# Weights stored block by block in order of use, and a fifth row of the memory output projection opened in the second score buffer

## The chip, the cores and the metric

The kernel runs on one core of one Trainium2 chip. The metric is the device time of one execution in microseconds (us), lower is better. A core has TensorE (PE, matrix products; PEld is its loading of the stationary operand), VectorE (DVE), ScalarE (ACT), GpSimd (POOL) and SyncE (SP), which here only issues transfers (DMAs) from the chip's memory (DRAM) to on-chip memory and back. Matrix products go into eight PSUM buffers of 128 x 512 float32.

## What is computed

Two layers of an encoder over 512 tokens of width 1024, with 256 memory tokens beside them. Each layer adds three things to x, and a last RMS norm follows:

```python
x = x + hybrid_mixer(rms_norm(x, norm_mix[l]), w_in[l], na_rpb[l],
                     gqa_q_norm[l], gqa_k_norm[l], w_out[l], rows, cos, sin)
x = x + memory_cross_attention(rms_norm(x, norm_mem_q[l]), rms_norm(mem, norm_mem_kv[l]),
                               w_mem_q[l], w_mem_kv[l], w_mem_o[l])
x = x + conv_ffn(rms_norm(x, norm_ffn[l]), w_up[l], conv_w[l], conv_b[l], w_down[l])
```

The mixer projects with w_in (1024 x 2304), runs eight heads of neighbourhood attention on an 8 x 64 grid and eight query heads of grouped attention over all tokens, and projects with w_out. The memory part is

```python
q = (h @ w_q).reshape(b, s, MEM_HEADS, MEM_HEAD_DIM)
sc = jnp.einsum('bqhd,bmhd->bhqm', q, k, preferred_element_type=jnp.float32) * (MEM_HEAD_DIM ** -0.5)
p = jax.nn.softmax(sc, axis=-1)
o = jnp.einsum('bhqm,bmhd->bqhd', p.astype(v.dtype), v).reshape(b, s, MEM_WIDTH)
return o @ w_o
```

with four heads of width 128, so the output projection sums over four k-steps of 128, one for each head. The feed-forward part projects to 2 x 2816 columns (w_up), convolves over three positions, gates, and projects back (w_down). Everything is float32.

## The kernel before

x is kept transposed, as eight tiles of 128 features x 512 tokens ("xT"). Each float32 factor is split into a high part and a low part in a reduced format (float32r), and a product is made of three: high x high, high x low, low x high (`mm3`, `gemm_T`). A 128 x 128 x 512 product is therefore three PE instructions of 512 columns.

**Weights.** `plan` lists all weight blocks in the order of their use, each with its DRAM source, its number of k-steps and of columns. A block is 512 KB (448 KB for blocks of w_down of seven k-steps). `emit_raw` loads it into one of two "raw" buffers (N_RAW) on SP's queue; `emit_split` makes the parts: ACT copies the high one ("hi<-raw"), POOL or DVE subtracts for the low one ("lo<-raw,hi"). Four pairs of hi and lo stand at a time (N_W). A raw buffer is free for the next load when its low part is made, so the load of a block goes out behind the split of the block two ahead of it. In DRAM the weights lie as the reference has them (w_in with reordered columns), and a block is cut out of a matrix: `cols` takes rows k0*128 on and columns c0 on, so one k-step of one partition is a piece of 512 B (128 columns), 1 KB (256) or 2 KB (512), and pieces follow each other at the pitch of the matrix: 9216 B for w_in, 22528 B for w_up, 4096 B for w_down and w_mem_kv. The four "outg" blocks of w_out are loaded in two halves of 64 partitions.

**The opening.** The first three weight blocks and x are loaded in slices (`FIRST`, `first_loads`): k-step 0 and 1 alone, then two k-steps at a time, with x's chunks between them, so that PE can start on the first slices. The two first slices of weights are issued by ACT, all else by SP.

**The memory part.** `mem_rows` makes the output projection: eight rows (128 output features x 512 tokens), each the sum of four k-steps, one for each head's output mo[0] to mo[3]. PSUM has four buffers named "mm", two named "sc" (scores) and two named "tr". While the heads are still worked on, rows 0 to 2 (N_ROWS = 3) are opened in "mm" buffers and get k-steps 0 to 2 as the heads become ready; row 3 is opened in an "sc" buffer. Then `mem_rows` waits for mo[3] (ACT copies its high part out of PSUM, DVE makes the low part). After that it walks over the rows: an opened row gets its last k-step, the others are opened in a free "mm" buffer and get all four. `Norm.close` then adds the row to xT, and makes the operands of the feed-forward part ("xg") and their squares, on DVE, ACT and POOL. Two rows share one block of w_mem_o.

**The order of the work.** The program is not issued as written. All calls go onto a tape (`Tape`, `Step`); a planner (`Tape.plan`, `run`, `due`) simulates it with a duration for each step, chooses an order for each engine among the steps that can start, and takes the best of nine such orders under small random delays. PE's order may differ from the tape by up to 300 of its own steps. `play` then issues the chosen order, and each engine executes its own list in that order. For a DMA the planner assumes 450 ns of issue, 1800 ns to land, and a transfer rate in `Step.__init__`: 205 GB/s for fewer than 128 partitions or within SBUF, 285 where a piece (the last dimension) is under 1 KB, 340 otherwise. Since all calls are issued from `play`, every instruction has the line of `take` or `play` in the profile (L376), and groups are told apart by their tiles.

Of the kernel before, what the change touches and what calls it, by code (L numbers as in the profile page):

```python
# [19 lines left out]
P = 128  # L20
# [48 lines left out]
    return n  # L69


def tag_of(tensor):
    return re.sub(r"(_\d+)+$", "", tensor.name)


class Step:
# [394 lines left out]
def encoder_kernel(ctx: ExitStack, tc: tile.TileContext, t: dict, out: list):  # L471
# [51 lines left out]


    def raw_tile():
        key, loads, nk, ncol, eng = plan[len(raws)]
# [5 lines left out]
        return raw, loads  # L532

    def emit_raw():
        raw, loads = raw_tile()
        for dst, src in loads:
            SP.dma_start(dst(raw), src)

    def emit_split(act=ACT, cuts=2):
        n = len(ready)  # L540
        key, loads, nk, ncol, eng = plan[n]
        raw = raws[n]
        raws[n] = None
        if key[0] in ("up", "down", "memq", "memo"):
            cuts = 1
        if eng[1:] == "r":
            hi, lo = rtile((nk, ncol)), rtile((nk, ncol))
        else:
            hi = wpool.tile([P, nk, ncol], F32R, tag="hi", name=nm("hi"))
            lo = wpool.tile([P, nk, ncol], F32R, tag="lo", name=nm("lo"))  # L550
        for i in range(cuts):
            k = slice(nk * i // cuts, nk * (i + 1) // cuts)
            act.copy(hi[:, k], raw[:, k])
            (POOL if eng[0] == "P" else DVE).tensor_sub(lo[:, k], raw[:, k], f(hi)[:, k])
        ready.append((hi, lo))
# [22 lines left out]
    def plan_up(l, j):  # L578
        cols(("up", j, 0), t["w_up"][l], 0, KC, P * j, P)
        cols(("up", j, 1), t["w_up"][l], 0, KC, D_FF + P * j, P)  # L580

    def plan_down(l, g):
        j0, nj = GROUPS[g]
        if l + 1 < DEPTH or g + 1 < len(GROUPS):
            for m in range(KC):
                cols(("down", g, m), t["w_down"][l], j0, nj, P * m, P)
            return
        for n, (k0, c0) in enumerate(((0, 0), (2, 0), (4, 0), (6, None), (0, 512), (2, 512), (4, 512))):
            eng = "P" if n < 2 else "Pr"
            if c0 is None:  # L590
                cols(("down", g, n), t["w_down"][l], j0 + k0, 1, 0, D, eng)
            else:
                cols(("down", g, n), t["w_down"][l], j0 + k0, 2, c0, 512, eng)

    def plan_wide(name, w, c0, eng="PPPP"):
        for kq in range(4):
            cols((name, kq), w, 2 * kq, 2, c0, 512, eng[kq])

    def plan_layer(l):
        w_in, w_out = t["w_in"][l], t["w_out"][l]  # L600
        for n, p in NA_ORDER:
            if n == "v":
                plan_wide("v", w_in, 1024, "DPDP")
            else:
                eng = {("q", 0): "Dx", ("k", 0): "Dx", ("q", 1): "Dx"}.get((n, p), "P") if l == 0 else "P"
                cols((n, p), w_in, 0, KC, (0 if n == "q" else 512) + P * p, P, eng)
        for kh in range(2):
            cols(("gkv", kh), w_in, 4 * kh, 4, 2048, 256)
        plan_wide("gq", w_in, 1536)
        for mp in range(4):  # L610
            cols(("outn", mp), w_out, 0, 4, 256 * mp, 256, "P")
        for m in range(4):
            cols(("memk", m), t["w_mem_kv"][l], 0, KC, P * m, P)
        plan_wide("memv", t["w_mem_kv"][l], 512)
        for mp in range(4):
            c = slice(256 * mp, 256 * mp + 256)
            plan.append((("outg", 0, mp), [
                (lambda r: r[0:64], w_out[512:768, c].rearrange("(k p) c -> p k c", p=64)),
                (lambda r: r[64:128], w_out[768:1024, c].rearrange("(k p) c -> p k c", p=64)),
            ], 4, 256, "P"))  # L620
        for h in range(4):
            cols(("memq", h), t["w_mem_q"][l], 0, KC, P * h, P)
        for mp in range(4):
            cols(("memo", 0, mp), t["w_mem_o"][l], 0, 4, 256 * mp, 256)
        for g, (j0, nj) in enumerate(GROUPS):
            for j in range(j0 + (g > 0), j0 + nj):
                plan_up(l, j)
            if g + 1 < len(GROUPS):
                plan_up(l, j0 + nj)
            plan_down(l, g)  # L630

    for l in range(DEPTH):
        plan_layer(l)

    def get_wide(name):
        return [get_w((name, kq), min(AHEAD, 3 - kq)) for kq in range(4)]
# [27 lines left out]
    for n in FIRST:  # L664
        if isinstance(n, slice):
            to = slice(n.start, n.stop + (n.stop == S))
            SP.dma_start(xg0[0][:, to], t["xT"][0:P, to])
        elif isinstance(n, int):
            SP.dma_start(xg0[n], t["xT"][n * P : (n + 1) * P, :])
        else:  # L670
            u, k0, nk = n
            if u == len(first_loads):
                first_loads.append(raw_tile())
            raw, loads = first_loads[u]
            (ACT if u < 2 and k0 == 0 else SP).dma_start(raw[:, k0 : k0 + nk], loads[0][1][:, k0 : k0 + nk])
# [172 lines left out]
    def mem_stat():  # L848

        acc = None  # L850
        for i in range(KC // 2):
            sq = tmp((2, MEMN))
            SP.dma_start(sq, t["memT"][i * 256 : (i + 1) * 256, :].rearrange("(k p) n -> p k n", p=P))
# [46 lines left out]
    for l in range(DEPTH):  # L900
# [560 lines left out]
        def mem_rows():  # L1461
# [231 lines left out]
    return np.ascontiguousarray(tab.astype(np.float32))  # L1693


def _in_order():

    order = _head_order()
# [58 lines left out]
```

## Time and profile before

| | |
|---|---|
| median of 3 runs | 1324.64 us (1323.74 to 1324.8) |
| profiled execution | 1324.17 us, of which the span is 1322.3 us |
| read from DRAM, written | 126.18 MB, 2.10 MB |
| packets of the hardware queue q1 | 197,808 with 135.84 MB |
| instructions | 17,751, of which 6,373 PE products |

Durations and times in the prediction come from the one profiled execution, and its times count from the span's start. In a row of a timeline the columns are start, duration, engine, operation, tiles written and read, shapes and count, and in brackets the idle time of the engine ahead of it with what ended it. "x3" means that three such instructions in a row are shown as one. A PE product's duration is from its start until its result has passed the array, so several overlap; the distance from one start to the next is what PE needs for each. In rows of waits the numbers are total us, times, and the longest.

### The profile page before, as it was taken

How to read it: one execution, taken by the hardware profiler on the slowest of the kernel's cores; microseconds unless marked ns; L12 is line 12 of the kernel's file. 1: busy time of each engine (PE TensorE's matmuls, PEld its weight loads, DVE VectorE, ACT ScalarE, POOL GpSimd, SP SyncE). 2: the span in 40 equal slices, each digit the busy share in tenths (PEclk: the TensorE clock that was granted, in tenths of full speed). 3: DMA queues.
4: the chain of work that ended last, by engine and by line, in shares of the span. 5: the costliest groups of instructions: out<-in, count | busy, mean ns of one | idle time of the engine just before them, and what ended most of it. 6: DMA issues, size and time to landing. Idle time of an engine off the chain costs nothing.

```text
span 1322.3 us, 17751 instructions
## 1 busy us (share of the span) xinstructions
PE 1313.2 (99%) x6373; PEld 1105.8 (84%) x6373; DVE 936.4 (71%) x1657; ACT 675.2 (51%) x1229; POOL 691.9 (52%) x481
## 2 busy tenths in 40 slices
PE   9999999999999999999999999999999999999998
PEld 7898888888888888888888988888888888888897
DVE  7679896776994488178445898866779835862875
ACT  6777786555442244144447867855644423432441
POOL 3565866726544444444636657775455444444451
PEclk9999999999999999999999999999999999999999
DMA  8661313322333333342355522233133333323331
GB/s 248 192 184 49 112 58 87 96 62 82 112 96 96 96 96 91 103 123 81 89 168 168 144 64 80 71 89 96 49 112 104 99 100 96 92 84 111 96 112 64
DMA packets 198327, 137.29 MB, mean 104 GB/s; under 512 B 5216, under 2 KB 185056, under 8 KB 198240
## 3 DMA queue, kind: packets, MB, share of 16 engines
q1 hardware_dynamic: 197808, 135.84, 35.1%
q8 instruction: 51, 0.84, 0.3%
q10 hardware_dynamic: 432, 0.33, 0.1%
q14 instruction: 36, 0.29, 0.1%
HBM read 126.18 MB, written 2.10 MB: 97 GB/s over the span
## 4 chain that ended last, share of the span: by engine, by line
PE 97%; ACT 1%; DVE 1%; POOL 0%; DMA 0%; issue 0%; SPq 0%; DVEq 0%; POOLq 0%; ACTq 0%
PE mm L376 86%; PE sc L376 6%; PE tr L376 4%; POOL lo L376 0%; DMA xT<-in_xT 0%; ACT hi L376 0%; ACT xg L376 0%; ACT t L376 0%; DVE r L376 0%; ACT r L376 0%; SPq L376 0%; DVE xg L376 0%; DVE t L376 0%; POOL t L376 0%; DVE s L376 0%
## 5 line engine op out<-in xcount | busy, mean ns | idle before, releaser
L376 POOL TENSOR_TENSOR lo<-raw,hi 128x1024 fp32r<-128x1024 f32 (+2 forms) x268 | 512.3, 1922 | 481.6 <-ACT hi L376 450.7
L376 PE MATMUL mm<-xg,hi 128*128 128x512 f32 (+1 forms) x1730 | 535.6, 390 | 0.8 <-ACT hi L376 0.8
L376 ACT CAST hi<-raw 128x512 fp32r<-128x512 f32 (+2 forms) x276 | 226.2, 839 | 354.7 <-PE mm L376 329.1
L376 PEld LDWEIGHTS mm<-xg,hi 128*128 128x128 f32 x1730 | 322.5, 188 | 65.9 <-ACT hi L376 1.0
L376 PE MATMUL mm<-xg,lo 128*128 128x512 f32 (+1 forms) x865 | 336.7, 389 | 0.0
L376 PE MATMUL mm<-r,hi 128*128 128x512 f32 (+1 forms) x1056 | 333.0, 390 | 0.4 <-ACT r L376 0.4
L376 DVE SCALAR_TENSOR_TENSOR t<-t,par,t 128x504 f32<-128x504 f32 (+1 forms) x352 | 281.3, 837 | 38.5 <-ACT t L376 36.5
L376 PEld LDWEIGHTS mm<-r,hi 128*128 128x128 f32 x1056 | 197.2, 188 | 40.3 <-ACT r L376 1.3
L376 PE MATMUL mm<-r,lo 128*128 128x512 f32 (+2 forms) x560 | 210.8, 376 | 0.0
L376 PEld LDWEIGHTS mm<-xg,lo 128*128 128x128 f32 x865 | 162.4, 188 | 33.7
L376 PEld LDWEIGHTS mm<-r,lo 128*128 128x128 f32 x560 | 105.2, 188 | 19.5
L376 DVE TENSOR_TENSOR xT<-xT,mm 128x512 f32<-128x512 f32 (+1 forms) x56 | 37.1, 667 | 111.8 <-PE mm L376 111.5
L376 PE MATMUL mm<-hi,xg 128*128 128x512 f32 (+1 forms) x384 | 107.7, 357 | 0.0
L376 POOL TENSOR_SCALAR t<-t,s 128x512 f32<-128x512 f32 (+1 forms) x112 | 66.7, 610 | 59.0 <-DVE s L376 52.5
L376 DVE TENSOR_TENSOR t<-mm,rep 128x512 f32<-128x512 f32 x88 | 60.1, 687 | 35.4 <-PE mm L376 35.2
L376 PE MATMUL sc<-r,r 128*128 128x256 f32 (+1 forms) x382 | 83.7, 336 | 0.0
L376 ACT ACTIVATE t<-sc,s,s 128x512 f32<-128x512 f32 (+1 forms) x96 | 67.9, 711 | 26.4 <-DVE s L376 25.0
L376 ACT ACTIVATE t<-t,par 128x512 f32<-128x512 f32 x88 | 70.8, 810 | 15.8 <-DVE t L376 15.8
L376 PEld LDWEIGHTS mm<-hi,xg 128*128 128x128 f32 x384 | 68.5, 189 | 9.4
L376 PE MATMUL tr<-ident,t 128*128 128x128 f32 x488 | 70.8, 272 | 0.3 <-POOL lo L376 0.3
L376 PEld LDWEIGHTS tr<-ident,t 128*128 128x128 f32 x488 | 59.3, 140 | 11.8 <-issue 0.8
L376 PE MATMUL mm<-lo,xg 128*128 128x512 f32 (+1 forms) x192 | 68.0, 356 | 0.0
(125 smaller groups left out, 1510.3 us busy)
## 6 DMA issues: line engine op xcount, KB each, us to landing
raw<-in_w_up SPq DMA_DIRECT2D x88, 512.0 KB, 3.9
raw<-in_w_in SPq DMA_DIRECT2D x33, 512.0 KB, 4.3
raw<-in_w_down SPq DMA_DIRECT2D x23, 512.0 KB, 4.0
raw<-in_w_down SPq DMA_DIRECT2D x24, 448.0 KB, 3.7
raw<-in_w_mem_kv SPq DMA_DIRECT2D x16, 512.0 KB, 4.0
r<-r SPq DMA_DIRECT2D x30, 256.0 KB, 3.5
r<-in_bias SPq DMA_DIRECT2D x16, 384.0 KB, 5.7
raw<-in_w_out SPq DMA_DIRECT2D x8, 512.0 KB, 3.5
```

Of the source, the lines that this page charges most:

```text
L376: call(*args, **kwargs)
```

## The change

There are two parts, and what the planner makes of them.

- The weights are put into one DRAM array "w", block by block in the order of use, each block as [128 partitions, k-steps, columns], so that the part of one partition lies in one run: 4 KB (3.5 KB for seven k-steps). A new function `weights()` lists the blocks, both for the host, which lays out the array, and for the kernel, which makes `plan` from it. Sizes, order and engines of the blocks stay; an "outg" block is one DMA instead of two. The slices of the opening are parts of these runs: k-step 0 and 1 alone are still pieces of 512 B, now at a pitch of 4 KB, and two k-steps are 1 KB. The memory tokens (memT) are laid out by partition as well.
- In `mem_rows` a second row, row 4, is opened in the other "sc" buffer with k-steps 0 to 2, ahead of the wait for mo[3].
- The planner's rates for a DMA go by the contiguous run (`run`) of both sides: 285 GB/s under 1 KB, 340 under 2 KB, 375 from 2 KB.

Cut to its core:

```diff
+def run(ap):
+    n = 1
+    for step, c in reversed(ap.ap[1:]):
+        if step != n:
+            break
+        n *= c
+    return n
...
-            short = min(4 * a.ap[-1][1] for a in (to, source) if a is not None) < 1024
+            runs = min(run(a) for a in (to, source) if a is not None)
             inside = source is not None and type(source.tensor).__name__ == type(to.tensor).__name__ == "Tile"
-            rate = 205.0 if to.shape[0] < P or inside else 285.0 if short else 340.0
+            rate = 205.0 if to.shape[0] < P or inside else 285.0 if runs < 256 else 340.0 if runs < 512 else 375.0
...
     def emit_raw():
-        raw, loads = raw_tile()
-        for dst, src in loads:
-            SP.dma_start(dst(raw), src)
+        SP.dma_start(*raw_tile())
...
-    def cols(key, w, k0, nk, c0, ncol, eng="P"):
-        src = w[k0 * P : (k0 + nk) * P, c0 : c0 + ncol].rearrange("(k p) c -> p k c", p=P)
-        plan.append((key, [(lambda r: r, src)], nk, ncol, eng))
...
+    at = 0
+    for key, name, l, rows, c0, ncol, eng in weights():
+        nk = rows.shape[1]
+        src = t["w"][at : at + P * nk * ncol].rearrange("(p k c) -> p k c", p=P, c=ncol)
+        plan.append((key, src, nk, ncol, eng))
+        at += P * nk * ncol
...
-            SP.dma_start(raw[i], t["memT"][i * 512 : (i + 1) * 512, :].rearrange("(k p) n -> p k n", p=P))
+            SP.dma_start(raw[i], t["memT"][:, 4 * i : 4 * i + 4])
...
-            m = N_ROWS
-            if m % 2 == 0:
-                w.append(get_w(("memo", 0, m // 2)))
-            rows.append((ps_s(), w[m // 2], slice(P * (m % 2), P * (m % 2) + P)))
-            gemm_T(*rows[m][:2], mo, range(3), 0, 3, rows[m][2])
+            for m in (N_ROWS, N_ROWS + 1):
+                if m % 2 == 0:
+                    w.append(get_w(("memo", 0, m // 2)))
+                rows.append((ps_s(), w[m // 2], slice(P * (m % 2), P * (m % 2) + P)))
+                gemm_T(*rows[m][:2], mo, range(3), 0, 3, rows[m][2])
+                yield
             yield lambda: mo[3] is not None
...
+def weights():
+    def cols(key, name, k0, nk, c0, ncol, eng="P"):
+        return key, name, l, np.arange(k0 * P, (k0 + nk) * P).reshape(nk, P).T, c0, ncol, eng
...
+    arrays["w"] = np.concatenate(
+        [a[name][l, rows][:, :, c0 : c0 + ncol].ravel() for _, name, l, rows, c0, ncol, _ in weights()])
```

More of the change, by code (lines that the diff above doesn't have):

```diff
@@ L525, in raw_tile @@
     def raw_tile():
-        key, loads, nk, ncol, eng = plan[len(raws)]
+        key, src, nk, ncol, eng = plan[len(raws)]
         if eng[1:] == "x":
@@ L531, in raw_tile @@
         raws.append(raw)
-        return raw, loads
+        return raw, src
     def emit_raw():
-        raw, loads = raw_tile()
-        for dst, src in loads:
-            SP.dma_start(dst(raw), src)
+        SP.dma_start(*raw_tile())
     def emit_split(act=ACT, cuts=2):
         n = len(ready)
-        key, loads, nk, ncol, eng = plan[n]
+        key, src, nk, ncol, eng = plan[n]
         raw = raws[n]
@@ L572, in get_w @@
         return w
-    def cols(key, w, k0, nk, c0, ncol, eng="P"):
-        src = w[k0 * P : (k0 + nk) * P, c0 : c0 + ncol].rearrange("(k p) c -> p k c", p=P)
-        plan.append((key, [(lambda r: r, src)], nk, ncol, eng))
[L578 to L630, printed above, removed]
@@ L632, in encoder_kernel @@
-    for l in range(DEPTH):
-        plan_layer(l)
+    at = 0
[4 more added lines that the diff above has]
+        at += P * nk * ncol
     def get_wide(name):
@@ L673, in encoder_kernel @@
                 first_loads.append(raw_tile())
-            raw, loads = first_loads[u]
-            (ACT if u < 2 and k0 == 0 else SP).dma_start(raw[:, k0 : k0 + nk], loads[0][1][:, k0 : k0 + nk])
+            raw, src = first_loads[u]
+            (ACT if u < 2 and k0 == 0 else SP).dma_start(raw[:, k0 : k0 + nk], src[:, k0 : k0 + nk])
     ACT.copy(small(1), ones)
@@ L1693, in _rope_tables, with wide, up @@
     return np.ascontiguousarray(tab.astype(np.float32))
+def weights():
+    def cols(key, name, k0, nk, c0, ncol, eng="P"):
+        return key, name, l, np.arange(k0 * P, (k0 + nk) * P).reshape(nk, P).T, c0, ncol, eng
+    def wide(key, name, c0, eng="PPPP"):
+        return [cols((key, kq), name, 2 * kq, 2, c0, 512, eng[kq]) for kq in range(4)]
+    def up(j):
+        return [cols(("up", j, i), "w_up", 0, KC, i * D_FF + P * j, P) for i in range(2)]
+    blocks = []
+    for l in range(DEPTH):
+        for n, p in NA_ORDER:
+            if n == "v":
+                blocks += wide("v", "w_in", 1024, "DPDP")
+            else:
+                eng = "Dx" if l == 0 and (n, p) in NA_ORDER[:3] else "P"
+                blocks.append(cols((n, p), "w_in", 0, KC, (0 if n == "q" else 512) + P * p, P, eng))
+        for kh in range(2):
+            blocks.append(cols(("gkv", kh), "w_in", 4 * kh, 4, 2048, 256))
+        blocks += wide("gq", "w_in", 1536)
+        for mp in range(4):
+            blocks.append(cols(("outn", mp), "w_out", 0, 4, 256 * mp, 256))
+        for m in range(4):
+            blocks.append(cols(("memk", m), "w_mem_kv", 0, KC, P * m, P))
+        blocks += wide("memv", "w_mem_kv", 512)
+        p = np.arange(P)[:, None]
+        rows = 512 + 256 * (p // HD) + HD * np.arange(4) + p % HD
+        for mp in range(4):
+            blocks.append((("outg", 0, mp), "w_out", l, rows, 256 * mp, 256, "P"))
+        for h in range(4):
+            blocks.append(cols(("memq", h), "w_mem_q", 0, KC, P * h, P))
+        for mp in range(4):
+            blocks.append(cols(("memo", 0, mp), "w_mem_o", 0, 4, 256 * mp, 256))
+        for g, (j0, nj) in enumerate(GROUPS):
+            for j in range(j0 + (g > 0), j0 + nj + (g + 1 < len(GROUPS))):
+                blocks += up(j)
+            if l + 1 < DEPTH or g + 1 < len(GROUPS):
+                blocks += [cols(("down", g, m), "w_down", j0, nj, P * m, P) for m in range(KC)]
+                continue
+            for n, (k0, c0) in enumerate(((0, 0), (2, 0), (4, 0), (6, None), (0, 512), (2, 512), (4, 512))):
+                at = (k0, 1, 0, D) if c0 is None else (k0, 2, c0, 512)
+                blocks.append(cols(("down", g, n), "w_down", j0 + at[0], *at[1:], "P" if n < 2 else "Pr"))
+    return blocks
 def _in_order():
@@ L1743 @@
     arrays["bias"] = rpb[:, :, ro, ci]
-    arrays["w_in"] = a["w_in"][:, :, _in_order()]
-    for n in ("w_out", "w_mem_q", "w_mem_kv", "w_mem_o", "w_up", "w_down"):
-        arrays[n] = a[n]
+    a["w_in"] = a["w_in"][:, :, _in_order()]
+    arrays["w"] = np.concatenate(
+        [a[name][l, rows][:, :, c0 : c0 + ncol].ravel() for _, name, l, rows, c0, ncol, _ in weights()])
     arrays = {f"in_{n}": np.ascontiguousarray(v) for n, v in arrays.items()}
```

4 lines of the change are left out of this document (2 added, 2 removed).

## The prediction

> **What bounds the kernel now.** I read the page first, then the waits of TensorE, the chain of waits, and last the timeline around the rows that the change moves. On the page the first part, busy shares, and the slices of part 2 say which engine sets the end:
>
> ```profile
> span 1322.3 us, 17751 instructions
> ...
> PE 1313.2 (99%) x6373; PEld 1105.8 (84%) x6373; DVE 936.4 (71%) x1657; ACT 675.2 (51%) x1229; POOL 691.9 (52%) x481
> ...
> PEclk9999999999999999999999999999999999999999
> ```
>
> TensorE (PE) is busy 1313.2 of 1322.3 us at full clock; no other engine is over 71%. So a transfer or a buffer is worth only what PE waits for it. All that PE waited for, by its own list of waits:
>
> ```profile
> PE tr L376 <- DVE ones L376: 1.0, 1, 1.0
> PE mm L376 <- ACT hi L376: 0.8, 1, 0.8
> PE mm L376 <- ACT r L376: 0.4, 2, 0.2
> PE tr L376 <- POOL lo L376: 0.3, 1, 0.3
> PE sc L376 <- DVE xg L376: 0.3, 1, 0.3
> ```
>
> That is 2.8 us in the whole run, and 1.0 of it lies ahead of the warm-up products. No row names a DMA. The list shows idle time, and a busy PE is not PE at its peak, so I need the pace. The chain of waits, in order of time, gives it:
>
> ```profile
> 126.35 5.47 PE mm L376 x24
> ...
> 211.71 37.91 PE mm L376 x167
> ...
> 317.47 342.84 PE mm L376 x1512
> ...
> 778.06 5.48 PE mm L376 x24
> ...
> 863.11 39.01 PE mm L376 x172
> ```
>
> In the feed-forward part of layer 0, 1512 products of 512 columns take 342.84 us: 0.2267 us from one start to the next, without a gap. A distance above 0.2267 between two such starts is a stall, listed or not. The Trainium skill ("Perfetto Trace Analysis", "Identifying the Most-Contended Engine") calls matmul busy time a bad measure of headroom and points to the weight-load share, which is 84% here; by that, PE could have 16% to spare. The trace does not bear it out: a gapless stretch at one pace leaves nothing there that earlier weights could fill.
>
> **The change, term by term.**
>
> *The fifth row.* mem_rows opens rows 0 to 2 of the memory output projection in "mm" buffers and row 3 in a score buffer ("sc"), three of four k-steps each; then PE needs mo[3], the last head's output. The timeline there, layer 0 and layer 1:
>
> ```profile
> 286.15 0.59 ACT L376 CAST r<-mm 128x512 fp32r<-128x512 f32 x1 [2.63 <-PE mm L376]
> 286.18 0.39 PE L376 MATMUL sc<-r,lo 128*128 128x512 f32 x1
> 286.77 0.69 DVE L376 TENSOR_TENSOR r<-mm,r 128x512 fp32r<-128x512 f32 x1 [2.53 <-ACT r L376]
> 286.79 0.96 PE L376 MATMUL mm<-r,hi 128*128 128x512 f32 x3 [0.22 <-ACT r L376]
> 287.58 0.40 PE L376 MATMUL sc<-r,hi 128*128 128x512 f32 x1
> ```
>
> ```profile
> 938.74 0.39 PE L376 MATMUL sc<-r,lo 128*128 128x512 f32 x1
> 939.35 0.96 PE L376 MATMUL mm<-r,hi 128*128 128x512 f32 x3 [0.22 <-ACT r L376]
> 940.15 0.40 PE L376 MATMUL sc<-r,hi 128*128 128x512 f32 x1
> ```
>
> Row 3 ends at 286.18. The next product starts 0.61 us later, after ACT's copy of mo[3]: 0.61 - 0.23 = 0.38 us lost. The next three take 0.79 us from start to start against 3 x 0.2267 = 0.68: 0.11 more. Layer 1 shows 0.61 and 0.80, the same. Stall: 0.49 us a layer, 0.98 in both. The added row has nine products, 9 x 0.2267 = 2.04 us of work that needs only mo[0..2]; mo[3] is complete at 287.46 (286.77 + 0.69), row 4 would run until 286.41 + 2.04 = 288.45. The stall is covered with 1.0 us to spare: **-0.98 us**. The products of row 4 are the same ones, earlier, so they add nothing.
>
> What could be late next? First, the third weight block of that projection, which row 4 reads:
>
> ```profile
> 272.23 2.39 POOL L376 TENSOR_TENSOR lo<-raw,hi 128x1024 fp32r<-128x1024 f32 x1 [6.46 <-ACT hi L376]
> ...
> 274.64 20.42 SPq L376 DMA_DIRECT2D raw<-in_w_up x3
> ...
> 288.75 2.00 ACT L376 CAST hi<-raw 128x1024 fp32r<-128x1024 f32 x2 [2.02 <-PE mm L376]
> ...
> 289.88 4.78 POOL L376 TENSOR_TENSOR lo<-raw,hi 128x1024 fp32r<-128x1024 f32 x2 [15.27 <-PE sc L376]
> ```
>
> With two raw buffers a load leaves when the split two blocks ahead of it is done. The load behind the split of 274.62 is already of w_up, so that split is of the third or fourth block; the third is there 11.8 us before row 4 wants it at 286.41. It costs nothing. Second, the first two w_up blocks: their splits (288.75 to 294.66) wait until rows 0 to 3 release the first weight buffers. Those rows now close up to 2.04 - 0.38 = 1.66 us later, so the splits end by 296.3, while PE reaches the feed-forward part at 300.59 - 0.49 = 300.1 (row below). Hidden, with 3.8 us to spare. Third, VectorE's closing of the rows, which makes that part's operands:
>
> ```profile
> 288.48 0.70 DVE L376 TENSOR_TENSOR mm<-mm,xT 128x512 f32<-128x512 f32 x1 [1.02 <-PE mm L376]
> ...
> 302.04 0.74 DVE L376 SCALAR_TENSOR_TENSOR xg<-mm,par,xg 128x512 fp32r<-128x512 f32 x1
> ```
>
> ```profile
> 300.59 0.62 PE L376 MATMUL mm<-xg,hi 128*128 128x512 f32 x2
> ```
>
> DVE works nearly without a break from 288.48. After the change row 0 is complete at about 288.45 + 3 x 0.2267 + 0.17 = 289.3, so this series starts 0.87 later and the operand of row 6 is done at 302.78 + 0.87 = 303.65. PE wants it 18 products into the new part, now at 304.67, then at 304.18. Half a microsecond stays; at the worst shift of 1.66 it would be 0.26 late. I take **+0.05** a layer, +0.1 in both, and keep 0 to +0.5 for the range.
>
> The wait for mo[3] itself is not new. Nothing queues for the second score buffer: its next user comes after the whole feed-forward part of the layer.
>
> *Contiguous weights.* Each block becomes one run of 4 KB a partition (3.5 KB for the seven-step ones) instead of pieces of 512 B to 2 KB; the two half loads of each "outg" block become one. The page's DMA issues:
>
> ```profile
> raw<-in_w_up SPq DMA_DIRECT2D x88, 512.0 KB, 3.9
> ...
> raw<-in_w_down SPq DMA_DIRECT2D x23, 512.0 KB, 4.0
> ...
> raw<-in_w_mem_o SPq DMA_DIRECT2D x8, 512.0 KB, 3.5
> ...
> r<-in_w_in SPq DMA_DIRECT2D x9, 128.0 KB, 4.1
> ```
>
> The same 512 KB lands in 3.9 in 512 B pieces (w_up) and in 3.5 in 1 KB pieces (w_mem_o), so a load gets perhaps 0.4 us shorter. Who would use that? The next load's own wait answers: SP's queue stands 1016.3 us behind POOL.
>
> ```profile
> SPq L376 <- POOL lo L376: 1016.3, 204, 17.3
> ```
>
> A raw block lands and then lies there until its split is due; PE waits for none. I cost this at nothing outside the opening. If the cover were gone (a load exposed in full), each block would cost up to 3.5 us; no row comes near.
>
> *The opening* is the one stretch where the DMA engines are the limit. Its row of the windows (busy time of PE, weight loads, DVE, ACT, POOL; clock, DMA share, GB/s), and the timeline in it:
>
> ```profile
> 0.00:25.00 25.00, 22.91 (x103) 18.79 (x104) 20.12 (x42) 18.43 (x39) 5.05 (x11) 1.00 0.93 287
> ```
>
> ```profile
> 5.83 0.30 ACT L376 CAST hi<-r 128x128 fp32r<-128x128 f32 x1 [1.09 <-DMA r<-in_w_in]
> ...
> 16.48 3.19 DVE L376 TENSOR_TENSOR t<-t,t 128x512 f32<-128x512 f32 x3
> ...
> 17.25 0.73 ACT L376 ACTIVATE xg<-xT 128x512 fp32r<-128x512 f32 x1
> ...
> 19.59 1.77 DVE L376 SCALAR_TENSOR_TENSOR xg<-xT,xg 128x512 fp32r<-128x512 f32 x1
> ...
> 21.42 0.19 PEld L376 LDWEIGHTS sc<-xg,hi 128*128 128x128 f32 x1 [0.72 <-DVE xg L376]
> ```
>
> DMA share 0.93 at 287 GB/s. PE loses 0.8 us to the first slice of the third weight (ACT at 5.83, PE's row "ACT hi"); that slice keeps its 512 B pieces, so nothing is gained for certain. It loses 0.3 us to "DVE xg": the last chunk of x is there at 17.2 (ACT takes it at 17.25), but its low part is made at 19.59, since DVE had three sums of squares ahead of it; PE wants it at 21.42 - 0.72 = 20.7. The planner's new rates put landings earlier, which may bring that split ahead of them. From below both waits vanish, -1.1; from above nothing happens. I take **-0.3**, nearest to the second row alone.
>
> *The order.* Every engine's order is planned anew, from a tape with two moved rows and other transfer rates. The trace cannot show that order. As a measure: the chain passes the same stretch of the global attention in both layers, 126.35 to 211.71 (85.36 us) and 778.06 to 863.11 (85.05): two plans of like work differ by 0.3 us. For four attention stages I allow 1.2 us to either side, and take 0.
>
> Sum: the profiled execution took 1324.17 us, 1.87 outside its span; -0.98 + 0.1 - 0.3 = -1.2 gives 1323.0. The median of the runs is 0.47 above that execution, so I forecast **1323.4 us**.
>
> **Rivals.**
>
> *Faster by more.* The opening loses both waits (-1.1), the row keeps its -0.98, and the new order gains the 1.2 us: -3.3, 1321.3. For it: the waits are there to take. Against: PE's list has only 1.8 us besides the first wait.
>
> *The wait moves.* The gate's stall goes, but DVE's late operands (+0.5), or the new order (+0.5), take it back: 1324.7, no change. That is also what it looks like if the planner had kept PE's order as it was: the tape only offers the earlier row.
>
> *Slower, by the planner's belief.* The opening runs at 287 GB/s, and the new rates are 340 and 375 for nearly everything. What has arrived when the last chunk of x is there, 17.2 us x 287 = 4.9 MB, a planner at 340 to 375 expects 2.7 to 4.0 us earlier (14.5 or 13.2 us). ACT and DVE take their instructions in order, so one conversion placed ahead of its data holds all behind it, and PE with them. It decides once the shift exceeds that chunk's slack, 20.7 - 17.2 = 3.5 us. The price is then up to the whole shift, 4.0, once: 1324.64 - 0.98 + 4.0 = 1327.7. Against it: the real rate rises too with longer pieces, and PE has not waited long for a transfer so far.
>
> *Slower, by the pitch.* The opening's slices are now read at a 4 KB pitch, a power of two, instead of 9 KB. w_down is read at a 4 KB pitch today, mostly in 512 B pieces, and lands in 4.0 against 3.9 for w_up: 0.1 us, no matter. But if those 1.5 MB went at half rate, the opening would get 1.5 MB / 287 = 5.2 us longer, and 5.2 less the 3.5 of slack is +1.7: with the row's gain, 1325.4. The Trainium skill ("DMA: Bandwidth & Descriptors", "Latency and other measured facts") reports such a halving for row pitches of 4 MiB, down from 512 KiB; the w_down row speaks against it at 4 KB.
>
> **How the numbers follow.** A measurement of this kernel can tell about 0.2% (2.65 us) from no change. Forecast, 1322.0 to 1324.2: 0.47. Wait moves, 1324.2 to 1325.2: 0.14. Faster by more, under 1322.0: 0.27. Slower by the planner, over 1327.3: 0.09. Pitch: 0.03. So faster 0.27, same 0.64, slower 0.09. The range 1320.8 to 1326.0 leaves out the planner's case (0.09) and the far third of the faster one (0.09).
>
> **What would show it.** The row of the opened rows in the score buffer, from the groups of PE by form:
>
> ```profile
> L376 PE MATMUL sc<-r,hi 128*128 128x512 f32 x16 | 5.6, 392 | 0.0
> ```
>
> In the changed profile these products double to 32, no 0.6 us step stands between the opened rows and mo[3] in either layer; mm<-ACT r leaves PE's waits. The hardware queue q1 falls from 197,808 packets to some 45,000 (an estimate: about 220 weight loads of 128 runs each, 28,000, and the rest as now), at the same megabytes, and blocks land in about 3.5 us. PE's busy time stays. The forecast is wrong if PE's pace of 0.2267 changes, if PE's waits name a DMA or "xg" after 300 us, or if the first 25 us hold fewer PE products than 103.

## The result, and the profile after

| kernel | median of 20 runs, us | range, us | profiled execution, us | span, us |
|---|---|---|---|---|
| before | 1323.44 | 1322.72 to 1324.80 | 1324.17 | 1322.3 |
| after | 1321.74 | 1321.25 to 1322.39 | 1321.62 | 1319.8 |

The ratio is 0.9986, with a 95% interval of 0.998 to 0.9992: 1.70 us faster, interval 1.1 to 2.6. In the profiled executions alone the difference is 2.55 us, because the one of before lies 0.73 above the median of its 20 runs. From the page of the changed kernel, the span, the busy shares and the queue:

```profile
span 1319.8 us, 17733 instructions
...
PE 1312.6 (99%) x6373; PEld 1107.1 (84%) x6373; DVE 940.5 (71%) x1657; ACT 675.7 (51%) x1229; POOL 692.1 (52%) x481
...
q1 hardware_dynamic: 42288, 135.83, 34.2%
...
raw<-in_w SPq DMA_DIRECT2D x192, 512.0 KB, 3.6
```

PE's busy time is nearly the same, 1312.6 against 1313.2; most of what went is idle time, 9.1 us before and 7.2 after. The packets fell from 197,808 to 42,288, at the same megabytes. Of PE's five rows of waits, one is left, the one ahead of the warm-up products:

```profile
PE tr L385 <- DVE ones L385: 1.0, 1, 1.0
```

And the groups of PE by form show the fifth row, 32 products where there were 16:

```profile
L385 PE MATMUL sc<-r,hi 128*128 128x512 f32 x32 | 10.2, 390 | 0.0
```

**Where the 2.55 us went.** Between the first product and the last, PE does the same work in both kernels, so I compared when it reaches the same amount of work. The distance between the two traces grows in four places and is level between them to within 0.1: 0.72 us in the opening, 0.66 from 90 us on (0.54 of it at 92 us, the rest by 150), 0.57 at the memory projection of layer 0 (0.05 of it behind the gate), 0.57 at that of layer 1: 2.5 in all. After the first 25 us this is no noise: the distance between two executions of before (its profile and the run e9 below) changes by 0.11 us at most over all later times.

*The gate.* Timelines of PE, ACT and DVE around mo[3], layer 0, and of PE in layer 1, changed kernel:

```profile
284.83 0.59 ACT L385 CAST r<-mm 128x512 fp32r<-128x512 f32 x1 [2.63 <-PE mm L385]
284.86 0.39 PE L385 MATMUL sc<-r,lo 128*128 128x512 f32 x1
285.09 0.62 PE L385 MATMUL sc<-r,hi 128*128 128x512 f32 x2
285.45 0.69 DVE L385 TENSOR_TENSOR r<-mm,r 128x512 fp32r<-128x512 f32 x1 [2.53 <-ACT r L385]
286.90 0.39 PE L385 MATMUL sc<-r,lo 128*128 128x512 f32 x1
287.13 0.62 PE L385 MATMUL mm<-r,hi 128*128 128x512 f32 x2
...
298.69 0.62 PE L385 MATMUL mm<-xg,hi 128*128 128x512 f32 x2
```

```profile
936.85 0.39 PE L385 MATMUL sc<-r,lo 128*128 128x512 f32 x1
937.07 0.61 PE L385 MATMUL sc<-r,hi 128*128 128x512 f32 x2
939.11 0.61 PE L385 MATMUL mm<-r,hi 128*128 128x512 f32 x2
```

Row 3 ends at 284.86, and row 4 starts 0.23 later, where before PE stood for 0.61. Row 4 lasts until 286.90; mo[3] was complete at 285.45 + 0.69 = 286.14, and its first product follows 0.23 behind row 4. The size can be checked by counting: from the last product of row 3 to the first of the feed-forward part there are 61 starts. They took 300.59 - 286.18 = 14.41 before and take 298.69 - 284.86 = 13.83 now, which is 61 x 0.2267. So 0.58 us were lost there, and nothing is.

*Near 90 us.* PE and DVE, first before and then after (in each fence PE, then DVE):

```profile
90.22 0.28 PE L376 MATMUL tr<-s,sel 128*128 128x8 f32 x2
91.07 0.40 PE L376 MATMUL mm<-hi,xg 128*128 128x256 f32 x2
91.81 0.63 PE L376 MATMUL tr<-ident,t 128*128 128x128 f32 x4 [0.34 <-POOL lo L376]
...
90.33 0.86 DVE L376 TENSOR_TENSOR t<-mm,t 64x256 f32<-64x256 f32 x2
91.22 0.45 DVE L376 STREAM_TRANSPOSE mem_rep<-tr 128x256 f32<-128x256 f32 x1
```

```profile
89.48 0.28 PE L385 MATMUL tr<-s,sel 128*128 128x8 f32 x2
90.33 0.40 PE L385 MATMUL mm<-hi,xg 128*128 128x256 f32 x2
90.57 0.60 PE L385 MATMUL tr<-ident,t 128*128 128x128 f32 x4
...
89.80 0.45 DVE L385 STREAM_TRANSPOSE mem_rep<-tr 128x256 f32<-128x256 f32 x1 [0.26 <-PE tr L385]
```

Here PE makes a small norm's factors ("tr<-s,sel"), DVE copies them out of their "tr" buffer ("mem_rep<-tr"), and PE wants a "tr" buffer for four transposes of t. Before, the transposes start 0.74 after the row of products ahead of them, now 0.24. The row of before blames POOL's "lo". But what also changed is DVE: before, two additions stood ahead of mem_rep, which started 1.0 us behind PE's product; now it starts 0.32 behind it. Which of the two it was, the traces cannot say: a run below does.

*The opening.* SP's queue there, before and after:

```profile
10.91 0.47 SPq L376 DMA_DIRECT2D raw<-in_w_in  x1
11.43 1.09 SPq L376 DMA_DIRECT2D xT<-in_xT  x1
```

```profile
10.23 0.33 SPq L385 DMA_DIRECT2D xT<-in_xT  x1
11.74 0.92 SPq L385 DMA_DIRECT2D raw<-in_w  x2
```

The new order issues x's last chunk ahead of the weight blocks, not behind one. ACT takes the chunk at 14.49 where it did at 17.25, DVE makes its low part at 16.04 where it did at 19.59, and PE's 0.3 us of "DVE xg" are gone. The place in the order is not all: before, that instruction of DVE also lasts 1.77 us, and 0.74 now. Run e3 below comes back to this.

### The profile page after: what moved, and what is told of

Read it like the earlier page. It is cut to its first block, busy times and chain, and to the rows that moved or that the text cites. A ratio compares the mean times of both kernels' runs of the same rounds, so it can differ in the third digit from the quotient of the medians.

```text
span 1319.8 us, 17733 instructions
## 1 busy us (share of the span) xinstructions
PE 1312.6 (99%) x6373; PEld 1107.1 (84%) x6373; DVE 940.5 (71%) x1657; ACT 675.7 (51%) x1229; POOL 692.1 (52%) x481
## 3 DMA queue, kind: packets, MB, share of 16 engines
q1 hardware_dynamic: 42288, 135.83, 34.2%
## 4 chain that ended last, share of the span: by engine, by line
PE 99%; ACT 0%; DVE 0%; issue 0%; ACTq 0%
PE mm L385 87%; PE sc L385 8%; PE tr L385 4%; ACT t L385 0%; ACT r L385 0%; DVE r L385 0%; DVE s L385 0%; DVE t L385 0%; DVE ones L385 0%; ACTq L385 0%; DVE mhalf L385 0%
## 5 line engine op out<-in xcount | busy, mean ns | idle before, releaser
L385 PE MATMUL mm<-r,hi 128*128 128x512 f32 (+1 forms) x1040 | 326.2, 389 | 0.0
L385 DVE SCALAR_TENSOR_TENSOR t<-t,par,t 128x504 f32<-128x504 f32 (+1 forms) x352 | 288.9, 858 | 38.7 <-ACT t L385 36.8
L385 PEld LDWEIGHTS mm<-r,hi 128*128 128x128 f32 x1040 | 194.5, 188 | 38.7
L385 PE MATMUL mm<-r,lo 128*128 128x512 f32 (+2 forms) x552 | 207.6, 376 | 0.0
```

The costliest lines, as they stand in the source:

```text
L385: call(*args, **kwargs)
```

## The experiments

Theory: the 2.5 us are the fifth row (1.1), and the new order: the step from 90 us on (0.66) and the opening (0.7). Faster transfers give nothing by themselves. Rivals: the contiguous transfers bring the opening's gain and more; the believed rates, not the layout, make the order; POOL's split is what PE waited for near 90 us; the opening's 0.7 is luck of one execution. Each kernel was timed beside before on the same chip, in five rounds of runs (11 runs of each kernel, 27 or 33 of before).

| run | kernel | median (range), us | before there | ratio (95%) |
|---|---|---|---|---|
| e1 | before + fifth row | 1321.96 (1321.50 to 1323.72) | 1323.32 | 0.9991 (0.9982 to 1.0) |
| e2 | after without fifth row | 1322.86 (1322.51 to 1323.21) | 1323.32 | 0.9995 (0.9987 to 1.0004) |
| e3 | after, planner's old rates | 1322.04 (1321.36 to 1323.41) | 1323.32 | 0.9989 (0.998 to 0.9997) |
| e4 | after, blocks in pieces | 1321.82 (1321.29 to 1323.23) | 1323.32 | 0.9989 (0.9981 to 0.9998) |
| e5 | after, all rates 285 | 1323.05 (1322.50 to 1324.12) | 1323.11 | 0.9999 (0.999 to 1.0008) |
| e6 | after, all rates 450 | 1324.68 (1323.31 to 1326.27) | 1323.11 | 1.001 (1.0001 to 1.0019) |
| e8 | after, unchanged | 1321.95 (1321.42 to 1322.29) | 1323.11 | 0.9989 (0.998 to 0.9998) |
| e9 | before, unchanged | 1323.48 (1322.76 to 1324.54) | 1323.11 | 1.0001 (0.9992 to 1.001) |
| e10 | e1 + mem_rep two places earlier | 1322.65 (1321.47 to 1323.60) | 1323.69 | 0.9989 (0.998 to 0.9998) |
| e11 | as e4 | 1321.71 (1321.24 to 1322.07) | 1323.69 | 0.9983 (0.9974 to 0.9992) |
| e12 | after, unchanged | 1321.90 (1321.68 to 1322.84) | 1323.69 | 0.9988 (0.9979 to 0.9997) |

The ratios' intervals are about 1.2 us to either side, so the steps of single traces, which repeat to about 0.1 us behind the opening, tell more than the medians.

### e1: the fifth row alone

```diff
-            m = N_ROWS
+            for m in (N_ROWS, N_ROWS + 1):
...
+                yield
```

> The kernel before with the fifth row alone: weights, pieces and the planner's rates stay. The orders differ from before's in some 200 places, nearly all in the two memory parts. Theory (three separate gains: the gate of the memory rows 1.05 us in both layers, the low part of x's last chunk in the opening about 0.55, a conversion near 90 us about 0.66, the latter two from the new order that the rates give): 1.0 us below before, the two gaps of 0.61 us ahead of the last head's products gone, the wait of 0.3 us on DVE xg and the one of 0.3 us on POOL lo still there. Rival (the row gains nothing by itself, the re-planned order does it all): same time as before.

1.36 us faster than before in the medians, with an interval that reaches no change, so the trace has to show the size. The chain of waits has a stretch of the same 1512 products in each layer, and exactly one gate, that of layer 1, between their starts. In e1, then in the changed kernel:

```profile
317.40 342.84 PE mm L376 x1512
...
969.38 333.91 PE mm L376 x1512
```

```profile
315.57 342.84 PE mm L385 x1512
...
967.55 333.91 PE mm L385 x1512
```

Both are 651.98 apart. Before has the first at 317.47 and the second here, which is 652.54 apart:

```profile
970.01 333.91 PE mm L376 x1512
```

The row gives 0.56 us in this layer wherever it is, whatever the order around it. The stall near 90 us stays in e1, as expected, and so does the wait on "DVE xg" (1.1 us here). But the row of the stall names something else than POOL:

```profile
PE tr L376 <- DVE mem_rep L376: 0.4, 1, 0.4
```

### e2: all but the fifth row

```diff
-            for m in (N_ROWS, N_ROWS + 1):
+            m = N_ROWS
...
-                yield
```

> The changed kernel with four opened rows, as before: new layout and rates alone. Theory: 1.0 us slower than the changed kernel, 0.7 us faster than before; the gaps of 0.61 us at the gate are back in both layers, the waits on DVE xg and on POOL lo stay gone. Rival (the layout and the rates bring all, the row is hidden anyway): as fast as the changed kernel.

0.46 us faster than before, not distinguishable from no change. In the trace the two starts of the chain lie 652.54 apart, as before (316.37 and 968.91), and the row "mm<-ACT r" stands in PE's waits again:

```profile
PE mm L385 <- ACT r L385: 0.4, 2, 0.2
```

The step from 90 us on is there in full: layout, rates and order bring these 0.66, and the row brings the two gates. By the medians e2 was expected 0.7 below before and lies 0.46 below.

### e3: the old rates in the planner

```diff
-            runs = min(run(a) for a in (to, source) if a is not None)
+            short = min(4 * a.ap[-1][1] for a in (to, source) if a is not None) < 1024
-            rate = ... 285.0 if runs < 256 else 340.0 if runs < 512 else 375.0
+            rate = ... 285.0 if short else 340.0
```

> The changed kernel with the planner's old rates (285 GB/s where the last dimension is under 1 KB, else 340), so nearly the order of e1, but with contiguous weights. Theory (the opening and the conversion near 90 us are won by the order, that is by the rates): 0.5 to 1.2 us slower than the changed kernel, and the same as e1; the waits on DVE xg and POOL lo come back. Rival (the transfers themselves are what is faster): as fast as the changed kernel, the waits gone.

Every block is read in runs of 4 KB, but the order on every engine is that of e1: the two traces have the same instructions in the same places (the "outg" loads, one instead of two, aside). So the pair e1 and e3 differs in the transfers alone. Behind 25 us e3 keeps one distance from e1, to within 0.1 us: the gain from 90 us on is lost, and "PE tr <- DVE mem_rep: 0.3" is back. So the 0.66 comes from the rates in the planner, by way of the order, not from the transfers. In time e3 is 0.1 us from e1; it was also expected 0.5 us or more above the changed kernel, and its median is 0.3 above.

The other wait, on "DVE xg", was expected back too and is not there. DVE, POOL and PE in e1, then DVE and POOL in e3:

```profile
20.06 1.85 DVE L376 SCALAR_TENSOR_TENSOR xg<-xT,xg 128x512 fp32r<-128x512 f32 x1
20.08 1.28 POOL L376 TENSOR_TENSOR lo<-raw,hi 128x512 fp32r<-128x512 f32 x1 [0.49 <-ACT hi L376]
21.96 0.50 PE L376 MATMUL sc<-xg,hi 128*128 128x512 f32 x1 [1.09 <-DVE xg L376]
```

```profile
19.23 0.74 DVE L385 SCALAR_TENSOR_TENSOR xg<-xT,xg 128x512 fp32r<-128x512 f32 x1
19.89 1.51 DVE L385 TENSOR_TENSOR lo<-r,hi 128x256 fp32r<-128x256 f32 x1
19.32 1.80 POOL L385 TENSOR_TENSOR lo<-raw,hi 128x512 fp32r<-128x512 f32 x1 [0.57 <-ACT hi L385]
```

In e1 the low part of x's last chunk takes 1.85 us while POOL splits a block. In e3 it is 0.09 us ahead of POOL's split and takes 0.74; POOL's split takes 1.80, and the next instruction of DVE 1.51, which takes 0.41 in e1 (at 21.83). The instruction takes 1.77 to 1.85 in the four profiles with blocks in pieces and an order like e1's here (before, e9, e1, e10) and 0.74 or 0.75 in the nine others. So the wait is one of DVE's instruction on POOL's as far as the rows show, and a shift of the transfers takes it away as well as the new order does. That the two engines hold each other up is how the planner counts such pairs (`shared` in `Step`); no run here tests it.

### e4 and e11: the changed order with blocks in pieces

```diff
-        src = t["w"][at : at + P * nk * ncol].rearrange("(p k c) -> p k c", p=P, c=ncol)
+        src = t["w"][at : at + P * nk * ncol].rearrange("(k p c) -> p k c", p=P, c=ncol)
...
-            runs = min(run(a) for a in (to, source) if a is not None)
+            runs = min(columns(a) if a.tensor.name == "in_w" else run(a) for a in (to, source) if a is not None)
```

A block is stored with its k-steps outermost, so that each transfer is cut into pieces of 512 B to 2 KB again, and the planner is told that it is not: every engine's order is that of the changed kernel.

> The changed kernel's order on PE, DVE, ACT, POOL and SP instruction for instruction, but each weight block lies in DRAM as [k-step, partition, column], so that its transfer is again cut into pieces of 512 B to 2 KB (and the opening's single k-steps are one contiguous 64 KB). Theory (the length of the pieces is hidden; only the order pays): within 0.3 us of the changed kernel, with some 195,000 packets on q1 and blocks landing in 3.9 instead of 3.6. Rival (contiguous runs pay): 0.5 to 1.3 us slower, with waits of PE on ACT hi, DVE xg or POOL lo in the first 100 us.

From the page of e4, the queue and the blocks:

```profile
q1 hardware_dynamic: 195632, 135.83, 35.3%
...
raw<-in_w SPq DMA_DIRECT2D x192, 512.0 KB, 4.1
```

A block lands in 4.1 us, not 3.6, and takes 195,632 packets; the time is that of the changed kernel, and its PE starts keep one distance from it after the opening, to within 0.06 us. Three of e4's 11 runs were over 1322.8 (the changed kernel's highest of 20 was 1322.39), so it was run once more:

> e4 once more, beside e12: the order of the changed kernel, weights cut into pieces again. Theory (pieces are hidden in the typical run): median within 0.2 us of e12; three of e4's eleven runs lay 1 us above its median, and if shorter transfers give the opening slack there are such runs here and none in e12. Rival (contiguous weights bring nothing, not even that): no more high runs here than in e12.

e11 has none of those, and 1321.71; e12 has one, at 1322.84. In e11's profile PE loses 0.2 us between 50 and 80 us that e4's does not lose. With 1321.74, 1321.95 and 1321.90 for the changed kernel, contiguous blocks gain nothing that these runs can tell, as between e1 and e3.

### e5 and e6: other beliefs, the same transfers

```diff
-            rate = ... 285.0 if runs < 256 else 340.0 if runs < 512 else 375.0
+            rate = ... 285.0
```

and the same with 450.0 for e6. The 205 for fewer than 128 partitions and for transfers within SBUF stays in both.

> The changed kernel, its planner told 285 GB/s for every DMA onto 128 partitions. SP then issues the block of weights ahead of x's last chunk again, as before. Theory (the order, not the transfers, makes what is left beside the row; slower rates put conversions later): the gain at the gate of 0.57 us a layer stays, x's last chunk lands after 17 us, and the step of 0.66 us near 90 us is lost: 0.5 to 1.0 us slower than the changed kernel. Rival (any new plan draws that step anew, true rates or not): anything within 1 us of it, with other stalls at other places.

> The changed kernel, its planner told 450 GB/s for every DMA onto 128 partitions, more than was ever measured here. SP issues x's last chunk ahead of the block, as in the changed kernel. Theory (the slower rival of the prediction: a planner that believes in earlier landings puts conversions ahead of their data): 1 us or more slower than the changed kernel, with waits of ACT for DMAs that PE feels in the first 25 us. Rival (there is slack of a raw buffer everywhere, belief costs nothing): within 0.4 us of the changed kernel.

e5 loses what the row gains: 1323.05. My expectation, that a planner with lower rates loses the step near 90 us, failed. That step is kept; instead two stalls of 0.8 and 0.5 us arise at 123 and at 182 us (PE waits for DVE's "t" and for POOL's "t"), and behind the opening the order costs 0.86 more than that of before, the row left out. e6 is 2.7 us slower than e8. In PE's timeline in layer 1:

```profile
738.66 0.74 PE L385 MATMUL sc<-r,r 128*128 128x256 f32 x4 [0.69 <-DMA r<-r]
```

A transfer inside SBUF ("r<-r"), issued at 730.4, is not there when the order has PE use it: it lands at 738.6. In e8 the same transfer goes at 727.5 and lands at 733.2. SP's queue in e6 has a third weight block ahead of it, which stands until 728.1 for POOL, and the transfers behind that block go out in one burst. PE loses 1.0 us there and another 0.8 at 183 us, waiting for POOL; in all this order costs 1.63 us behind the opening. In the first 25 us, where waits for DMAs were expected, PE has one of 0.4 us on DVE. That fits the rival "by the planner's belief", later in the run, but only in part: the assumed rate within SBUF is 205 GB/s in every version, so it can only be the belief in the other transfers, by way of SP's order, and no run separates that from a chance order.

### e8, e9 and e12: both kernels again

> The changed kernel once more, unchanged, beside the kernel before and e5, e6. Theory: after the first 25 us every product of PE starts at the same distance as in its first profile, to 0.05 us; only the opening differs, by up to 0.5 us. 1.6 to 1.8 us below before. Rival (the stages drift from run to run, the steps at the gate and near 90 us are chance): steps of other sizes.

> The kernel before once more, measured against itself. Theory: ratio 1, all stalls after 25 us as in its first profile (0.6 us at the gate twice, 0.5 us near 91 us); the opening differs, and its 0.7 us on the low part of x's last chunk may be larger or gone. Rival: the stalls after 25 us differ too, so that they belonged to one execution.

> The changed kernel a third time, unchanged, beside e10 and e11. Theory: 1.5 to 1.8 us below before, all runs within 1 us of each other as in both measurements so far, and the same distances of PE's products after 25 us.

The medians repeat: 1321.95 and 1321.90 after, 1323.48 before. The differences repeat less well: e8 is 1.16 us below the before timed with it, and 1.6 to 1.8 were expected; e12 is 1.79 below, and its runs span 1.16 us, not 1. Behind the opening all PE starts repeat, with one distance to within 0.11 us. The first 10 us do not. The changed kernel's profile and e12, PE in the opening:

```profile
6.71 0.41 PE L385 MATMUL sc<-xg,lo 128*128 128x256 f32 x1
6.93 0.42 PE L385 MATMUL sc<-xg,hi 128*128 128x256 f32 x2
7.19 0.28 PE L385 MATMUL sc<-xg,lo 128*128 128x256 f32 x1
7.31 0.40 PE L385 MATMUL mm<-xg,hi 128*128 128x256 f32 x2
```

```profile
9.32 0.60 PE L385 MATMUL sc<-xg,lo 128*128 128x512 f32 x1
9.75 0.63 PE L385 MATMUL sc<-xg,hi 128*128 128x512 f32 x2
10.22 0.39 PE L385 MATMUL sc<-xg,lo 128*128 128x512 f32 x1
```

A product of 256 columns starts every 0.21 us until 7.1 and every 0.12 behind that; in e12 products of 512 columns go at 0.43 at first, and at 0.23 from 10.0 on. So PE runs at half pace at first, and the end of that differs from execution to execution. The granted clock of the windows is 1.00 throughout, but the traces' own clock records agree with the starts: the first record, of full clock, begins at 4.1 us in e8, 4.8 in the profile of before, 5.6 in e4, 6.8 in e9, 7.0 here, 9.8 in e12 and 10.3 in e10, and there is none ahead of it, which the windows count as 1.00.

This is a part of what an execution gains or loses in the first 15 us, not all. At 12 us the changed kernel's three profiles lie up to 1.2 us apart, with the latest full clock (e12) last; but e8, with the earliest, is 0.4 behind the first profile, since PE then waits for slices (0.6 us of idle time between 4.4 and 8.9 us).

From 15 us to 50 us, in contrast, the changed kernel gains 0.59 us on the profile of before, and so do e8, e12 and e4 (0.59 to 0.60; e11 0.52): the low part of x's last chunk, which PE never waits for in these. That wait costs e9 0.1 us more than the profile of before, and e1 0.8 more. It costs e10, which has e1's order here, nothing: e10 is at half pace until 10.3 us, PE arrives 1.85 us later than in e1, and the low part is there. So the medians need not show the gain.

### e10: mem_rep ahead of the two additions

```diff
-        return best[1]
+        return self.early(best[1])
```

`early` moves DVE's instruction "mem_rep<-tr" ahead of the two DVE additions in front of it, in the order of e1, and leaves all else.

> e1 (the kernel before with the fifth row) with one instruction of DVE moved: near 90 us DVE makes mem_rep from a score-transposition buffer (tr) ahead of two additions of the neighbourhood attention instead of behind them. All other orders are those of e1, the weights and pieces those of before. Theory (the 0.63 us step there is PE waiting for that tr buffer, which DVE frees 1.0 us after the products that fill it; the POOL row that the profile names only ended at the same time): the step goes, 0.6 us below e1 after 100 us, and from 25 us on every product of PE stands as in the changed kernel. Rival (PE waits for the low part of a weight block that POOL makes then): the step stays, time as e1.

PE, DVE and POOL of e10 near 92 us (in this order):

```profile
91.23 0.28 PE L386 MATMUL tr<-s,sel 128*128 128x8 f32 x2
92.08 0.40 PE L386 MATMUL mm<-hi,xg 128*128 128x256 f32 x2
92.32 0.60 PE L386 MATMUL tr<-ident,t 128*128 128x128 f32 x4
...
91.55 0.45 DVE L386 STREAM_TRANSPOSE mem_rep<-tr 128x256 f32<-128x256 f32 x1
91.92 1.28 DVE L386 TENSOR_TENSOR t<-mm,t 64x256 f32<-64x256 f32 x3
...
89.05 3.78 POOL L386 TENSOR_TENSOR lo<-raw,hi 128x512 fp32r<-128x512 f32 x3 [0.34 <-ACT hi L386]
```

The transposes start 0.24 behind the products ahead of them, without a stall, while POOL's "lo" is busy until 92.83. So PE never waited for it: the wait was for the "tr" buffer that DVE frees, and the row "PE tr <- POOL lo" named a split that ended at about the same time. PE gains 0.54 us on e1 there, as much as the changed kernel gains at this place. Some 0.17 come back at 96 to 98 us; I take it that the additions are now late there, which no run shows. Net, the move gives 0.42, and 0.6 was expected; the other 0.12 of the 0.66 belong to other places of the new order. The median, 1.04 us below before, cannot be told from e1's. None of the versions beats the changed kernel by more than the runs can tell.

## Why the prediction was right, point by point

The direction and the range held: 1321.74 measured, 1323.4 forecast within 1320.8 to 1326.0; 1.70 us gained, 1.2 forecast. That the range held says little, since it is wide enough for no change at all (1323.44). The anchor was the weaker part: three runs of before gave a median of 1324.64, twenty gave 1323.44, so the profiled execution that the sum starts from was above the median, not below it, and the time I forecast is that of the kernel before. Taken from 1323.44, the sum would have given 1322.2. The nearness of the sum is in part luck: it has the row about right, the opening too small and the order's 0.66 not at all, while the medians show 0.7 less than the steps of the traces (below). The terms are the better test.

*The fifth row, -0.98: right, and 0.16 too small.* Measured: -0.57 a layer, -1.14. The working counted two late stretches up to 287.58, 0.49 us. The 57 starts behind it took 13.01 us to 300.59, where 57 x 0.2267 are 12.92: the 0.09 that was missing, spread over many products of which none is a wait. The cover was as predicted: mo[3] was complete 286.90 + 0.23 - 286.14 = 1.0 us before PE wanted it.

*VectorE's closing, +0.1: it did not come.* The shift was there. DVE's first closing in the changed kernel:

```profile
288.01 0.70 DVE L385 TENSOR_TENSOR mm<-mm,xT 128x512 f32<-128x512 f32 x1 [1.86 <-PE mm L385]
```

It leads the feed-forward part by 298.69 - 288.01 = 10.68 us, where before it led by 300.59 - 288.48 = 12.11: 1.43 later against PE, and 0.87 + 0.49 = 1.36 were forecast (the 0.87 should be 0.82 by its own working, 289.3 - 288.48). But no product waited for it: the start of the 1512 products comes 16.88 us behind the first product of the feed-forward part, before (317.47 - 300.59) as after (315.57 - 298.69). The other two covers held as well, since PE's waits name neither weights nor splits.

*Contiguous transfers at nothing: right.* Packets were forecast at some 45,000 and are 42,288; blocks at about 3.5 us, and they are 3.6. e4 and e11 undo it without effect in the changed order, and e1 and e3 have the same median in the old one. Where the cover is thin, in the opening, the transfers do move a wait (e3), but not the median.

*The opening, -0.3: the step happened, 0.59 in the traces, and the medians do not show it.* The split of the last chunk came ahead of the sums of squares, as guessed, and the wait for "DVE xg" went; besides, SP issues that chunk earlier, which I had not thought of. I read the wait as DVE's place in its order alone. The row that I quoted (19.59, 1.77 us) says more: at the 0.74 us that the same instruction takes elsewhere it would have ended at 20.33, ahead of the 20.7 at which PE wants it. The other wait that I counted, 0.8 for "ACT hi", belongs to that one execution: e9, the same kernel, has none. In the medians the three steps would make -1.14 - 0.66 - 0.59 = -2.39, against -1.70 measured (interval 1.1 to 2.6). What is missing lies in the first 15 us, if it is anywhere; which part of them stays open. I read the stretch as limited by DMA at a clock of 1.00; the rows of PE's starts show that PE itself was slow for part of it.

The Trainium skill has this in "TensorE: Matmul & The Clock Gate", "Part 1: The HAM clock gate (the "warmup" mystery)": TensorE begins at half clock and gets the full one after about 3.4 us of sustained work, at a moment that varies by some 0.5 us to either side. The trace agrees on the factor (0.21 against 0.12 us for 256 columns). It does not agree on the moment: PE's first product is at 1.04 in the changed kernel, and the full clock begins between 4.1 and 10.3 us over these profiles.

*The order, 0 within 1.2: the size was right, and the gain inside it was missed.* It gave -0.66. The row for most of it stood in the list of waits that I quoted, as "PE tr <- POOL lo 0.3", and no term took it up. Its listed 0.3 is little more than half of the 0.54 that it cost, and its releaser was wrong.

*Rivals.* "Faster by more" (1321.3) was nearest to the measured time, for the reason that it named, an order that gains; the forecast's own interval began at 1322.0, so the measured time lies in that of this rival, to which I gave 0.27. "The wait moves": not here, but e5 is that case, 1323.05 with the gate's stall gone. "Slower, by the planner's belief": not at 340 and 375; at 450 (e6) slower, and in a transfer within SBUF in layer 1 rather than in the opening, with the mechanism shown in part. "Slower, by the pitch": no sign of it. e4 reads the opening's slices of 512 B packed one behind the other, without the 4 KB pitch, and is no faster.

## What to carry to other kernels

Where one engine is busy 99% of the time, look for the starts that lie further apart than its pace, count what independent work could fill them, and move that work there: the 0.57 us a layer was worth what the count says and did not depend on the rest. Count from one fixed instruction to another (61 starts, 13.83 us), since the list of waits showed less than half of the loss. A new order from a planner is a draw of its own, from -0.66 to +1.63 us here, so test an edit with the order held fixed. And compare the length of an instruction that is waited for with that of its like elsewhere: 1.77 us against 0.74 was in the rows from the start.

## What the runs showed of the hardware

- PE runs the first products at half pace until 4.1 to 10.3 us after the start, a different time in each execution, though the windows' granted clock shows 1.00 there.
- 512 KB land in 3.6 us in runs of 4 KB and in 4.1 in pieces of 512 B to 2 KB, at 42,288 against 195,632 packets; with two buffers ahead, the difference is not seen in the time.
- A row of waits can name a releaser that ends at the same time as the true one: POOL's "lo" stood for DVE's copy out of a PSUM buffer.
- An instruction of DVE that runs beside a split of POOL took 1.77 to 1.85 us, and 0.74 where POOL's split began behind it; then the split took 1.80, not 1.28.
